# Keys and queries turned by VectorE in 32x32 blocks after a trip through DRAM, and sums of the output projection that wait for the heads

## The chip, the core and the metric

The kernel runs on one core of a Trainium2 chip. The core has five engines with a queue each, which works strictly in order: TensorE (PE; its weight loads are listed as PEld), VectorE (DVE), ScalarE (ACT), GpSimd (POOL) and SyncE (SP), which here only issues transfers. ScalarE issues transfers too, from the same queue that holds its casts. Instructions of different engines are ordered by semaphores alone. The metric is the device time of one execution in microseconds; lower is better.

## The reference

Two layers of a diffusion backbone over 256 latent tokens and 256 context tokens, 2048 channels wide, in float32. Layer 0 projects both streams by one wide matrix and runs two kinds of heads side by side: 16 attention heads of width 128 (keys and queries are normalised per head; scores of the 256 latent keys get a bias and a window mask, the 256 context keys none) and 8 groups of a state-space scan in both directions. Their gated outputs are concatenated, projected by `w_out`, gated and added to x. Layer 1 is a gated short convolution with its own two projections. Cut to what matters here:

```python
q = rms_norm(heads(cols(p, COL_Q, ...)), q_norm_g)      # 256 tokens x 16 heads x 128
k = rms_norm(heads(cols(p, COL_K, ...)), k_norm_g)      # latent, and kc from the context
s = einsum('qhd,khd->hqk', q, [k, kc]) * dh ** -0.5 + bias, masked
ya = softmax(s) @ [v, vc] * silu(gate_a)
yb = group_rmsnorm((ssd(...) + d * xs) * silu(z)) * g
x = x + gate * (concatenate([ya, yb]) @ w_out)          # then layer 1
```

## The kernel before

Every float32 product of a projection is made of three matmuls on rounded pairs: activations are split into `hH` and `hL`, weights into `wH` (a cast by ScalarE, L409) and `wL` (the rest, a subtraction by VectorE, L416). Weight tiles of 128x1024 come by SP's queue into five `raw` buffers and are split three tiles ahead (`wH0..2`, `wL0..2`). TensorE runs through the weight tiles in a fixed order: keys, values and queries of head quarter 0, then gates and the state-space columns of quarter 0, then for each quarter a = 1, 2, 3 queries, keys, gates, values and state-space columns, then `w_out` in three passes (the first over two column blocks), then layer 1.

What stands between the weight tiles is written as Python generators (`kq_gen`, `head_gen`, `make_x`, `group_gen`, `mix_gen`, `res_gen` and others). Each yields what it waits for, and a planner (`Plan`, `pump`, `force`) with its own table of costs decides after each small batch of projection matmuls whose next instructions are put into the queues. Three lists (`urgent`, `side`, `back`) are tried in this order. Where the projection itself needs something that no generator has made yet, `force` puts in the generators' instructions one after another, with no projection row between. Ten buffers `tmp` (128x512) and nine `half` (128x256) are shared under a budget: a generator begins or grows only while the budget has room.

The generators that the change and the prediction touch, with lines of the kernel before:

- `kq_gen` (L930): for each 128-token tile of keys (4) or queries (2) of a quarter, ScalarE squares the four heads (L936), VectorE and GpSimd make the inverse roots (L554, L555), VectorE scales the tile into a `tmp` (L945), and once the heads of the quarter before are done (`attn`), TensorE turns the four 128x128 squares (L202, four to a tile). ScalarE copies a key tile into `KT` (L962), VectorE scales a query tile by `gqk` into `QT` (L964). So there are 24 tiles in all.
- `head_gen` (L995): casts and low parts of the head's keys and queries (L1041 to L1045), two halves of scores, softmax, four turns for each half, their split into `PH` and `PL` (L1065, L1067), values (L1074, L1076), the product PV and the gate (L1087). The output goes to DRAM (`mixd`, L921).
- `group_gen` (L1335): for each of two halves and two heads, decay rows are loaded from DRAM (`csr`, L1356), shifted by ScalarE (L1366), subtracted by VectorE (L1370), raised by ScalarE (L1373), masked products are made (L1376 on ScalarE, L1381 and L1384 on VectorE), and TensorE multiplies them with `xtm`; sums and gates (L1396, L1398), squares (L1400). Then the group norm: L1407, a small matmul, L1418, GpSimd L1420, L1424, a matmul, L1434, and the write to `mixd`.
- `mix_gen` (L1511): a pair of 128x256 blocks is read back from `mixd` by a transfer that ScalarE issues (L1516) and split (L1521, L1522) into `mix0` to `mix31`, the activations of the output projection. Blocks 0 to 15 come from the heads, 16 to 31 from the state groups; the projection takes them in the order 0 to 11, 16 to 31, 12 to 15.
- `res_gen` (L1541): loads gate row and x for a 512-column block, gates the projection's sum and adds x. It held four `tmp` from the ninth of the sixteen steps of a pass on.

Of the kernel before, what the change touches and what calls it, by code (L numbers as in the profile page):

```python
# [37 lines left out]
class Plan:  # L38
# [32 lines left out]
    def cost(self, e, op, i, ins, outs):  # L71
        n = max(self.size(a) for a in ins + outs)
        if e == "PE":
            n, cols = self.size(outs[0]), outs[0].ap[0][1]
            if i.is_transpose:
                return n / 1.2 + 3, 190
            if ins[0].dtype == F32R:
                return 9 + 0.434 * n, 190
            return 2 * max(55, n / 1.2) * (0.27 if cols == 32 else 0.52 if cols == 64 else 1) + (80 if cols < 128 else 0), 190
        if e == "DVE":  # L80
            if op == "Memset":
                return n * 0.26 + 60, 90
            if op in ("Reciprocal", "TensorReduce"):
                return n * 1.04 + 70, 90
            if len([a for a in ins if self.size(a) >= n]) >= 2 or op == "ISA" or self.psum(ins):
                return n * 1.22 + 70, 90
            return n * 0.6 + 130, 90
        if e == "ACT":
            return n * 0.85 + 150 + (200 if len(outs) > 1 else 0), 100
        if e == "POOL":  # L90
            return (n * 186 if n < 70 else n * 2.4) + 150, 60
        return 60, 0
# [49 lines left out]
def kernel(ctx: ExitStack, tc, x, cx, ada_w, ada_b, w_in, w_out, sc_in, sc_out, rpb, small, const,  # L142
# [57 lines left out]
    def turn(o, i):  # L200
        k = i.shape[0]
        E(T.transpose(o, i, ident if k == 128 else ident[:k, :k]))  # L202


    urgent, side, back = [], [], []
    got = set()
# [720 lines left out]

    attn = [0]

    def kq_gen(key, a, ps, nt, stat, dst, banked):  # L930

        for t in range(nt):
            yield W_("ACT", ps[t])
            jk = tmp()
            for h in range(4):
                E(S.activation(jk[:, h * 128:h * 128 + 128], ps[t][:, h * 128:h * 128 + 128], AF.Square,  # L936
                               accum_out=stat[:, 4 * t + h:4 * t + h + 1]))
            give(free_t, jk)
        yield W_("DVE", stat)
        rstd(stat[:, :4 * nt], stat[:, :4 * nt], 128, EPS, 4 * nt)  # L940
        kns = {}

        def norm(t):
            kn = kns[t] = tmp()
            E(V.tensor_tensor(out=four(kn), in0=ps[t].rearrange("p (h d) -> p h d", h=4),  # L945
                              in1=stat[:, 4 * t:4 * t + 4].unsqueeze(2).to_broadcast([128, 4, 128]), op=ALU.mult))
            if banked:
                give(free_b, ps[t])

        for t in range(nt):  # L950
            yield W_("DVE", stat)
            norm(t)
        yield when(lambda: not (attn[0] < 8 * (a if key else 0)))
        for t in range(nt):
            yield W_("PE", kns[t], nb=1)
            pt = bank()
            for h in range(4):
                turn(pt[:, h * 128:(h + 1) * 128], kns[t][:, h * 128:(h + 1) * 128])
            give(free_t, kns[t])
            yield W_("ACT" if key == "K" else "DVE", pt)  # L960
            if key == "K":
                E(S.copy(dst[:, :, t * 128:(t + 1) * 128], four(pt)))  # L962
            else:
                E(V.tensor_scalar(out=dst[:, :, t * 128:(t + 1) * 128], in0=four(pt), scalar1=gqk, scalar2=None, op0=ALU.mult))  # L964
            give(free_b, pt)
        got.add((key, a))

    def v_gen(a, ps):
# [26 lines left out]
    def head_gen(a, h):  # L995
# [43 lines left out]
        yield ("grow", 2, 0)  # L1039
        yield W_("ACT", KT[:, h, :], QT[:, h, :])  # L1040
        E(S.copy(kH, KT[:, h, :]))  # L1041
        E(S.copy(qH, QT[:, h, :]))
        yield W_("DVE", kH)
        E(V.tensor_tensor(out=kL, in0=KT[:, h, :], in1=kH.bitcast(F32), op=ALU.subtract))
        E(V.tensor_tensor(out=qL, in0=QT[:, h, :], in1=qH.bitcast(F32), op=ALU.subtract))  # L1045
        yield W_("PE", kL, qL, nb=1)
        p0 = score(0)
        yield W_("DVE", p0)
# [489 lines left out]
    passed = set()  # L1538
    at = [0]

    def res_gen(k, c0, ps):  # L1541
        cols = slice(c0, c0 + 512)
        yield when(lambda: n_back[0] >= 3)
        yield W_("SP", mrow[0:1])
        g2 = []
        for t in range(2):
            yield when(lambda: at[0] >= 9 + 3 * t or k in passed)
            gb, xr = tmp(), tmp()
            E(DMA.dma_start(gb, mrow[0, cols].partition_broadcast(128)))
# [129 lines left out]
    kcol = 0  # L1679
    for ns in ((0, 512), (1024,), (1536,)):  # L1680
        pss = [banks(2) for n in ns]
        for ip in range(16):
            at[0] = ip
            if ip >= 14:
                reserve[0] = 2
            if ip == 8:
                for k, (n, ps) in enumerate(zip(ns, pss)):
                    spawn(urgent, res_gen(kcol + k, n, ps), 4)
            force(lambda: mH[2 * order[ip] + 1] is not None)
            hold[0] = len(passed) == 3 and ip >= NTAIL  # L1690
            if hold[0]:

                if ip > NTAIL:
                    continue
                force(lambda: all(mH[2 * order[q] + 1] is not None for q in range(NTAIL, 16)))
                ws = [use(q) for q in range(16 - NTAIL)]
                spawn(urgent, norm_gen(), 0, 1)
                for t in range(2):
                    for q, (H, Lo) in enumerate(ws):
                        for b in range(2):  # L1700
                            i = 2 * order[NTAIL + q] + b
                            mm_act([pss[0][t]], mH[i][:, 0, t * 128:(t + 1) * 128], mH[i][:, 1, t * 128:(t + 1) * 128],
                                   H[:, b], Lo[:, b], False, NTAIL + q == 15 and b == 1)
# [181 lines left out]
```

## Time and profile before

| | before |
|---|---|
| median of 3 runs (lowest to highest) | 1805.11 us (1805.0 to 1809.3) |
| profiled execution, its own time | 1800.62 us |
| its span | 1798.8 us |
| TensorE busy / idle in the span | 1765.1 / 33.7 us |
| VectorE, ScalarE busy | 1302.0, 796.7 us |
| turns of a `tmp` by TensorE (L202) | 324, of which 96 belong to `kq_gen` |
| granted TensorE clock | 0.999 |

The profile describes one execution, which the profiler recorded. Busy times are taken as the union of an engine's instructions; matmuls overlap each other, so that the time a matmul costs TensorE is the distance of its start from the next start, not its duration. Issues of transfers and waits in an engine's queue are not busy time. In rows by time the columns are start, time from the first start to the last end of the row, engine, line, operation, output and inputs, count, and in brackets the idle time before it with what ended it. In rows by stretch the columns are the stretch, its length, and the busy time of PE, PEld, DVE, ACT and POOL with the instruction counts, then granted clock, DMA share and GB/s.

### The profile page before, as it was taken

How to read it: one execution, taken by the hardware profiler on the slowest of the kernel's cores; microseconds unless marked ns; L12 is line 12 of the kernel's file. 1: busy time of each engine (PE TensorE's matmuls, PEld its weight loads, DVE VectorE, ACT ScalarE, POOL GpSimd, SP SyncE). 2: the span in 40 equal slices, each digit the busy share in tenths (PEclk: the TensorE clock that was granted, in tenths of full speed). 3: DMA queues.
4: the chain of work that ended last, by engine and by line, in shares of the span. 5: the costliest groups of instructions: out<-in, count | busy, mean ns of one | idle time of the engine just before them, and what ended most of it. 6: DMA issues, size and time to landing. Idle time of an engine off the chain costs nothing.

```text
span 1798.8 us, 26647 instructions
## 1 busy us (share of the span) xinstructions
PE 1765.1 (98%) x10057; PEld 1493.6 (83%) x10057; DVE 1302.0 (72%) x2121; ACT 796.7 (44%) x1410; POOL 31.1 (2%) x28
## 2 busy tenths in 40 slices
PE   6999999999999999999999999999999999999998
PEld 4677888888888879888888898888878888888887
DVE  5566777878686877685875787787657777777665
ACT  5322544436252455242454343654445444444442
POOL 0000100001000000000001000000000000000000
PEclk9999999999999999999999999999999999999999
DMA  9987654566656556655574566878857777877564
GB/s 343 343 289 256 194 168 126 156 205 196 201 171 190 156 184 200 191 157 167 171 218 119 163 190 194 233 218 286 282 182 229 242 247 226 263 224 247 188 210 153
DMA packets 249217, 376.92 MB, mean 210 GB/s; under 512 B 32656, under 2 KB 104048, under 8 KB 249088
## 3 DMA queue, kind: packets, MB, share of 16 engines
q1 hardware_dynamic: 239792, 366.64, 65.5%
q10 hardware_dynamic: 9296, 8.57, 1.4%
q8 instruction: 79, 1.29, 0.3%
q14 instruction: 50, 0.41, 0.1%
HBM read 368.70 MB, written 7.77 MB: 209 GB/s over the span
## 4 chain that ended last, share of the span: by engine, by line
PE 91%; DMA 3%; DVE 3%; issue 1%; ACT 1%; SPq 0%; POOL 0%; POOLq 0%; DVEq 0%; ACTq 0%
PE bank L198 89%; PE bank L202 3%; DMA tmp<-dram_csr 2%; DVE wL L416 1%; DMA raw<-in_ada_w 0%; DMA tmp<-dram_mixd 0%; DVE acc L803 0%; DMA tmp<-in_x 0%; DVE hL L752 0%; SPq L566 0%; DVE tmp L1381 0%; DVE tmp L1200 0%; ACT wH L409 0%; DVE half L1396 0%; DVE tmp L748 0%
## 5 line engine op out<-in xcount | busy, mean ns | idle before, releaser
L409 ACT CAST wH<-raw 128x1024 fp32r<-128x1024 f32 (+1 forms) x440 | 459.1, 1044 | 684.7 <-PE bank L198 585.5
L416 DVE TENSOR_TENSOR wL<-raw,wH 128x1024 fp32r<-128x1024 f32 (+1 forms) x440 | 531.9, 1214 | 227.0 <-ACT wH L409 224.3
L198 PE MATMUL bank<-h,wH 128*128 128x512 f32 x1024 | 358.7, 395 | 2.7 <-ACT h L1664 1.5
L198 PE MATMUL bank<-hH,wH 128*128 128x256 f32 (+1 forms) x1040 | 343.2, 330 | 0.9 <-ACT wH L409 0.9
L198 PE MATMUL bank<-hL,wH 128*128 128x256 f32 (+1 forms) x1040 | 337.2, 324 | 0.0
L198 PE MATMUL bank<-hH,wL 128*128 128x256 f32 (+1 forms) x1024 | 331.7, 324 | 1.1 <-DVE wL L416 1.1
L198 PE MATMUL bank<-h,wL 128*128 128x256 f32 x1024 | 287.2, 280 | 0.1
L198 PE MATMUL bank<-wH,hH 128*128 128x512 f32 x640 | 257.4, 403 | 4.8 <-ACT hH L746 2.6
L198 PE MATMUL bank<-wL,hH 128*128 128x512 f32 x640 | 250.1, 391 | 0.3 <-DVE wL L416 0.3
L198 PE MATMUL bank<-wH,hL 128*128 128x512 f32 x640 | 249.8, 391 | 0.1
L803 DVE SCALAR_TENSOR_TENSOR acc<-raw,csil,acc 128x512 f32<-128x512 f32 x256 | 191.8, 749 | 59.8 <-DMA raw<-in_ada_w 45.4
L198 PEld LDWEIGHTS bank<-h,wH 128*128 128x128 f32 x1024 | 192.2, 188 | 48.4 <-issue 2.6
L198 PEld LDWEIGHTS bank<-hH,wH 128*128 128x128 f32 x1040 | 197.9, 190 | 18.7 <-issue 2.0
L198 PEld LDWEIGHTS bank<-hL,wH 128*128 128x128 f32 x1040 | 198.0, 190 | 15.4
L198 PEld LDWEIGHTS bank<-hH,wL 128*128 128x128 f32 x1024 | 194.8, 190 | 17.5 <-DVE wL L416 2.1
L198 PEld LDWEIGHTS bank<-h,wL 128*128 128x128 f32 x1024 | 193.6, 189 | 0.4 <-DVE wL L416 0.4
L198 PE MATMUL bank<-wH,mix 128*128 128x512 f32 x512 | 162.8, 393 | 0.0
L198 PEld LDWEIGHTS bank<-wH,hH 128*128 128x128 f32 x640 | 120.3, 188 | 35.3 <-issue 6.6
L198 PEld LDWEIGHTS bank<-wH,hL 128*128 128x128 f32 x640 | 120.2, 188 | 25.4 <-DVE hL L752 0.6
L198 PEld LDWEIGHTS bank<-wL,hH 128*128 128x128 f32 x640 | 120.3, 188 | 24.6 <-DVE wL L416 1.1
L198 PEld LDWEIGHTS bank<-wH,mix 128*128 128x128 f32 x512 | 96.2, 188 | 20.7 <-issue 0.9
L198 PE MATMUL bank<-wL,mix 128*128 128x512 f32 x256 | 99.9, 390 | 0.0
(259 smaller groups left out, 1790.1 us busy)
## 6 DMA issues: line engine op xcount, KB each, us to landing
raw<-in_w_in SPq DMA_DIRECT2D x209, 512.0 KB
raw<-in_ada_w SPq DMA_DIRECT2D x163, 512.0 KB
raw<-in_sc_in SPq DMA_DIRECT2D x128, 512.0 KB
raw<-in_w_out SPq DMA_DIRECT2D x64, 512.0 KB
raw<-in_sc_out SPq DMA_DIRECT2D x32, 512.0 KB
tmp<-dram_csr SPq DMA_DIRECT2D x32, 256.0 KB
PT<-in_ada_w SPq DMA_DIRECT2D x14, 512.0 KB
yi<-in_ada_w SPq DMA_DIRECT2D x8, 512.0 KB
```

Source lines behind the costliest of these rows:

```text
L198: E(T.matmul(o, l, r, start=start, stop=stop, skip_group_check=True))
L202: E(T.transpose(o, i, ident if k == 128 else ident[:k, :k]))
L409: E(S.copy(H, v))
L416: E(V.tensor_tensor(out=Lo, in0=v, in1=H.bitcast(F32), op=ALU.subtract))
L803: E(V.scalar_tensor_tensor(out=acc, in0=v[:, j], scalar=csil[:, 2 * k + j:2 * k + j + 1], in1=acc, op0=ALU.mult, op1=ALU.add))
```

## The change

The tile that VectorE scales is now written with its 32-column blocks in another order (`mixed`, `plain`), goes to a DRAM buffer `kqd`, issued from ScalarE's queue (L968 of the changed kernel), and comes back two tiles at a time into one buffer `kqD` by four transfers of 32 partitions each (`fetch`, L212), also from ScalarE's queue, so that each 32x32 block lies where its turned form belongs. VectorE then turns all blocks of a tile with one instruction (`blocks`, L217) straight into `KT` or `QT`. A flag `kqbusy` lets one fetch be under way at a time. The scaling of queries by `gqk` moves into the head's cast and low part, and the tile's buffer is given back when the write is issued. The sums of the output projection (`res_gen`) are entered without a claim on buffers; they begin when all heads and groups are done and then claim four `tmp`.

```diff
+    mixed = lambda ap: ap.rearrange("p (b k i) -> p k b i", b=4, k=4)
+    plain = lambda ap: ap.rearrange("p (k b i) -> p k b i", b=4, k=4)
+    def fetch(dst, src):
+        n = src.shape[0] // 32
+        for b in range(4):
+            E(DMA2.dma_start(dst[32 * b:32 * b + 32].rearrange("p t (a x) -> p (t a) x", a=4),
+                             bass.AP(tensor=src.tensor, offset=src.offset + 128 * b, ap=[[512, 32], [32 * 512, n], [1, 128]])))
+    def blocks(o, i):
+        E(V.transpose(o.rearrange("p k (a j) -> p a k j", a=4), i.rearrange("p (a k j) -> p a k j", a=4, k=4)))
...
-            E(V.tensor_tensor(out=four(kn), in0=ps[t].rearrange("p (h d) -> p h d", h=4),
-                              in1=stat[:, 4 * t:4 * t + 4].unsqueeze(2).to_broadcast([128, 4, 128]), op=ALU.mult))
+            E(V.tensor_tensor(out=mixed(kn), in0=plain(ps[t]),
+                              in1=stat[:, 4 * t:4 * t + 4].unsqueeze(2).unsqueeze(3).to_broadcast([128, 4, 4, 32]), op=ALU.mult))
...
+            yield W_("AQ", kn)
+            E(DMA2.dma_start(src[t * 128:(t + 1) * 128], kn))
+            give(free_t, kn)
+        yield ("cap", 0, 0)
         yield when(lambda: not (attn[0] < 8 * (a if key else 0)))
-        for t in range(nt):
-            yield W_("PE", kns[t], nb=1)
-            pt = bank()
-            for h in range(4):
-                turn(pt[:, h * 128:(h + 1) * 128], kns[t][:, h * 128:(h + 1) * 128])
-            give(free_t, kns[t])
-            yield W_("ACT" if key == "K" else "DVE", pt)
-            if key == "K":
-                E(S.copy(dst[:, :, t * 128:(t + 1) * 128], four(pt)))
-            else:
-                E(V.tensor_scalar(out=dst[:, :, t * 128:(t + 1) * 128], in0=four(pt), scalar1=gqk, scalar2=None, op0=ALU.mult))
-            give(free_b, pt)
+        for t in range(0, nt, 2):
+            yield when(lambda: not kqbusy)
+            kqbusy.append(1)
+            yield W_("AQ", src[t * 128:(t + 2) * 128])
+            Dk = st([128, 2, 512], "kqD", name=f"kqD_{key}{a}{t}")
+            fetch(Dk, src[t * 128:(t + 2) * 128])
+            for k in range(2):
+                yield W_("DVE", Dk)
+                blocks(dst[:, :, (t + k) * 128:(t + k + 1) * 128], Dk[:, k])
+            kqbusy.pop()
...
-        E(S.copy(qH, QT[:, h, :]))
+        E(S.mul(qH, QT[:, h, :], gqk))
...
-        E(V.tensor_tensor(out=qL, in0=QT[:, h, :], in1=qH.bitcast(F32), op=ALU.subtract))
+        E(V.scalar_tensor_tensor(out=qL, in0=QT[:, h, :], scalar=gqk, in1=qH.bitcast(F32), op0=ALU.mult, op1=ALU.subtract))
...
+    side_left = lambda: [t for t in side if t.gen.__name__ in ("head_gen", "group_gen")]
     def res_gen(k, c0, ps):
-        yield when(lambda: n_back[0] >= 3)
+        yield when(lambda: n_back[0] >= 3 and attn[0] == 32 and not side_left())
+        yield ("grow", 4, 0)
...
-                    spawn(urgent, res_gen(kcol + k, n, ps), 4)
+                    spawn(urgent, res_gen(kcol + k, n, ps))
```

The planner's own cost of the block turn is entered as that of a reduction of the same size. Since the planner sees other instructions and other free buffers, it orders most generators' work anew from the first keys on. Three places matter below.

The first is TensorE's queue during the gates of quarter 0, where the keys of quarter 0 are turned (`const` holds the identity, `tmp` the scaled tile):

```order
 L198 MATMUL bank_124<-hL_992,wH_136 128x256
 L198 MATMUL bank_124<-hH_987,wL_139 128x256
-L202 MATMUL bank_130<-const,tmp_109 128x128 x4
-L202 MATMUL bank_129<-const,tmp_110 128x128 x4
-L202 MATMUL bank_130<-const,tmp_112 128x128 x4
 L198 MATMUL bank_123<-hH_1128,wH_137 128x256
 L198 MATMUL bank_123<-hL_1133,wH_137 128x256
```

The groups of four turns are gone and nothing stands in their place; over the whole queue 24 such rows go, and every other row is kept, many at another place.

The second is TensorE's queue at the last two state groups (6 and 7) in the first pass of the output projection. Before, the last group's products with `xtm`, its sum of squares (`half7`) and its norm (`half8`) stand apart, with rows of the projection (`mix`) between:

```order
L198 MATMUL bank7_130<-wH2_138,mix19_9248 128x512
L198 MATMUL bank4_127<-tmp5_109,xtm_147 64x128
...
L198 MATMUL bank1_124<-wH2_138,mix19_9248 128x512
...
L198 MATMUL bank0_123<-const_153,half7_121 128x1 x2
L198 MATMUL bank7_130<-wH1_137,mix21_9307 128x512
...
L198 MATMUL bank2_125<-wH2_138,mix23_9242 128x512
L198 MATMUL bank3_126<-half8_122,const_153 128x128 x2
L198 MATMUL bank7_130<-wH0_136,mix22_9239 128x512
```

In the changed kernel:

```order
L198 MATMUL bank5_128<-wH1_137,mix27_9210 128x512
L198 MATMUL bank3_126<-tmp1_105,xtm_147 64x128
...
L198 MATMUL bank7_130<-PH_1686,vH_1690 128x256
...
L198 MATMUL bank6_129<-tmp8_112,xtm_147 64x128
...
L198 MATMUL bank4_127<-tmp4_108,xtm_147 64x128
...
L198 MATMUL bank3_126<-const_153,half4_118 128x1 x2
L198 MATMUL bank7_130<-half8_122,const_153 128x128 x2
L198 MATMUL bank6_129<-tmp2_106,xtm_147 64x128
...
L198 MATMUL bank4_127<-const_153,half5_119 128x1 x2
L198 MATMUL bank3_126<-half6_120,const_153 128x128 x2
L198 MATMUL bank2_125<-wH2_138,mix28_9950 128x512
```

All four products of groups 6 and 7 (four rows each), the product PV of the last head and both norms now stand between the last row of mix27 and the first of mix28, and no row of the projection among them.

The third is ScalarE's queue ahead of mix28, the first block of group 6. Before, the read of its pair (into `tmp6`) is issued ten rows ahead of the cast; in the changed kernel it stands behind the writes of both groups:

```order
L935 DMA dram_mixd_1684<-half1_115 128x256
L935 DMA dram_mixd_1684<-half0_114 128x256
L1416 ACTIVATE half2_116<-half3_117 128x256
L935 DMA dram_mixd_1684<-half7_121 128x256
L1532 DMA tmp1_105<-dram_mixd_1684 128x2x256
L935 DMA dram_mixd_1684<-half3_117 128x256
L1532 DMA tmp5_109<-dram_mixd_1684 128x2x256
L1537 CAST mix28_9950<-tmp1_105 128x256
```

The read into `tmp1` holds group 6 alone (`half1` and `half0`), but it is issued after the write of `half7`, which is group 7's.

More of the change, by code (lines that the diff above doesn't have):

```diff
@@ L82, in cost @@
                 return n * 0.26 + 60, 90
-            if op in ("Reciprocal", "TensorReduce"):
+            if op in ("Reciprocal", "TensorReduce", "StreamTranspose"):
                 return n * 1.04 + 70, 90
@@ L928 @@
     attn = [0]
+    kqd = drt([4, 768, 512], "kqd")
+    kqbusy = []
     def kq_gen(key, a, ps, nt, stat, dst, banked):
@@ L940, in kq_gen @@
         rstd(stat[:, :4 * nt], stat[:, :4 * nt], 128, EPS, 4 * nt)
-        kns = {}
-        def norm(t):
-            kn = kns[t] = tmp()
-            E(V.tensor_tensor(out=four(kn), in0=ps[t].rearrange("p (h d) -> p h d", h=4),
-                              in1=stat[:, 4 * t:4 * t + 4].unsqueeze(2).to_broadcast([128, 4, 128]), op=ALU.mult))
+        src = kqd[a, 512 * (key == "Q"):512 * (key == "Q") + 128 * nt]
+        for t in range(nt):
+            yield W_("DVE", stat)
+            kn = tmp()
+            E(V.tensor_tensor(out=mixed(kn), in0=plain(ps[t]),
+                              in1=stat[:, 4 * t:4 * t + 4].unsqueeze(2).unsqueeze(3).to_broadcast([128, 4, 4, 32]), op=ALU.mult))
             if banked:
                 give(free_b, ps[t])
-        for t in range(nt):
-            yield W_("DVE", stat)
-            norm(t)
+            yield W_("AQ", kn)
+            E(DMA2.dma_start(src[t * 128:(t + 1) * 128], kn))
+            give(free_t, kn)
+        yield ("cap", 0, 0)
         yield when(lambda: not (attn[0] < 8 * (a if key else 0)))
-        for t in range(nt):
-            yield W_("PE", kns[t], nb=1)
-            pt = bank()
-            for h in range(4):
-                turn(pt[:, h * 128:(h + 1) * 128], kns[t][:, h * 128:(h + 1) * 128])
-            give(free_t, kns[t])
-            yield W_("ACT" if key == "K" else "DVE", pt)
-            if key == "K":
-                E(S.copy(dst[:, :, t * 128:(t + 1) * 128], four(pt)))
-            else:
-                E(V.tensor_scalar(out=dst[:, :, t * 128:(t + 1) * 128], in0=four(pt), scalar1=gqk, scalar2=None, op0=ALU.mult))
-            give(free_b, pt)
+        for t in range(0, nt, 2):
[8 more added lines that the diff above has]
+            kqbusy.pop()
         got.add((key, a))
```

## The prediction

> **What bounds the kernel now.** I read the page's busy table and its slices first, then the busy time by stretch, to see where TensorE is not working.
>
> ```profile
> span 1798.8 us, 26647 instructions
> PE 1765.1 (98%) x10057; PEld 1493.6 (83%) x10057; DVE 1302.0 (72%) x2121; ACT 796.7 (44%) x1410; POOL 31.1 (2%) x28
> PE   6999999999999999999999999999999999999998
> ...
> core 0: us, PE busy (x) PEld busy (x) DVE busy (x) ACT busy (x) POOL busy (x), PEclk, DMA share, GB/s
> 0.00:100.00 100.00, 79.09 (x575) 55.34 (x576) 57.86 (x139) 45.20 (x93) 2.91 (x10) 1.00 0.96 335
> ...
> 300.00:400.00 100.00, 100.00 (x585) 86.04 (x584) 84.30 (x148) 46.52 (x91) 2.07 (x1) 1.00 0.58 173
> ...
> 1100.00:1200.00 100.00, 99.14 (x497) 82.28 (x496) 80.78 (x166) 58.92 (x122) 0.73 (x1) 1.00 0.74 217
> ...
> 1300.00:1360.00 60.00, 56.59 (x295) 46.84 (x294) 36.61 (x57) 28.04 (x43) 1.11 (x2) 1.00 0.59 188
> ...
> 1600.00:1799.00 199.00, 193.40 (x998) 164.62 (x996) 125.98 (x160) 83.34 (x108) 0.00 (x0) 0.99 0.64 204
> ```
>
> TensorE is the bound. It is idle 21 us in the first 100, 3.4 us around 1340 and 5.6 us in the last stretch; elsewhere there is hardly a gap, at granted clock 1.00. So two things alone can move the end: TensorE work that goes away, and new holes in TensorE. Other engines' added work costs nothing unless it makes a hole. This holds as long as the order gives TensorE something to do while a head or a state group runs its long chain on VectorE and ScalarE, as between 1100 and 1200.
>
> **What is removed.** 24 groups of four turns on TensorE (16 of keys, 8 of queries), a copy by ScalarE behind each key group and a scaling by VectorE behind each query group. One group among matmuls of 256 columns, and the two followers:
>
> ```profile
> 215.20 0.29 PE L198 MATMUL bank<-hH,wL 128*128 128x256 f32 x1
> 215.32 0.60 PE L202 MATMUL bank<-const,tmp 128*128 128x128 f32 x4
> 215.68 0.36 PE L198 MATMUL bank<-hH,wH 128*128 128x256 f32 x1
> 215.88 0.28 PE L198 MATMUL bank<-hL,wH 128*128 128x256 f32 x1
> ...
> L962 ACT COPY KT<-bank x16: 585/588/599, 216.0 to 978.0; 128x512 f32<-128x512 f32 x16
> ...
> L964 DVE TENSOR_SCALAR QT<-bank,gqk x8: 742/746/752, 223.2 to 916.6; 128x512 f32<-128x512 f32 x8
> ```
>
> Starts are what counts, since ends overlap. From 215.32 to 215.68 the turns hold TensorE 0.36 us, and the next step takes 0.20 in place of 0.12, so a group costs 0.44 us, and 24 of them 10.6 us. TensorE is the bound there, so this is the gain: **-10.6 us**.
>
> **What is added, off the path.** VectorE gets 24 block transposes, which this trace does not have. The nearest rows of a 128x512 tile are 0.69 (the row at 1156.71 below) and 0.75 us (L964), so 16.6 to 18 us; 6.0 us of scaling goes away. Net some 11 us, spread over 200 to 1000, where VectorE is at most 84% busy (300 to 400): hidden by TensorE's matmuls, and 11 us if that cover were gone. The scaling that moves into a head's cast and low part makes no new instruction. ScalarE loses 16 x 0.59 = 9.4 us and issues 24 writes and 48 fetches at about 0.38 us each (L1516 below), 27 us: net +18 us on an engine 47% busy in its 100 us row. These issues wait in its queue for VectorE's product or for the write's landing, and the weight casts stand behind them. Three weight tiles, each 12 matmuls of 0.23 us or 2.8 us, are ready ahead, so a late transfer must exceed some 8 us to reach TensorE; the landings below end at 7.4. I take 0, and 7 us as the upper bound (twelve fetches at about 0.6). Of bytes, 12.6 MB more pass at a DMA share of 0.58.
>
> **What is moved.** The order is made anew by the planner, and this is where I expect the loss. In the changed order, TensorE has no projection row between the first row of the state groups' last products (tmp1) and mix28: the two groups' chains and the last head's product stand alone, and mix28 needs a read that ScalarE issues behind the write of half7, the end of the second group's chain. Before, 18 rows or more of output projection stood behind each step of the last group. VectorE's list runs in order from the first masked product of tmp1 to the scaling of half7, and cannot start early: it stands behind the softmax of head 15, which needs scores that TensorE made 24 matmuls earlier. Its prices:
>
> ```profile
> 388.38 0.64 DVE L1381 SCALAR_TENSOR_TENSOR tmp<-tmp,dtl,tmp 128x128 f32<-128x128 f32 x2 [0.78 <-ACT tmp L1376]
> 389.05 0.43 DVE L1384 TENSOR_TENSOR tmp<-tmp 128x256 f32<-128x256 f32 x1
> 396.64 1.22 DVE L416 TENSOR_TENSOR wL<-raw,wH 128x1024 fp32r<-128x1024 f32 x1
> 399.22 0.42 DVE L1396 TENSOR_TENSOR half<-bank,yi 128x256 f32<-128x256 f32 x1
> 399.67 0.42 DVE L1398 TENSOR_TENSOR half<-half,sz 128x256 f32<-128x256 f32 x1
> 414.92 0.42 DVE L1407 TENSOR_TENSOR half<-half,half 128x256 f32<-128x256 f32 x1
> 418.15 0.15 DVE L1418 TENSOR_SCALAR r<-bank 128x2 f32<-128x2 f32 x1
> 418.22 0.74 DVE L803 SCALAR_TENSOR_TENSOR acc<-raw,csil,acc 128x512 f32<-128x512 f32 x1
> 419.55 0.48 DVE L1424 TENSOR_SCALAR half<-const,r 128x128 f32<-128x128 f32 x2 [0.59 <-POOL r L1420]
> 420.94 0.87 DVE L1434 SCALAR_TENSOR_TENSOR half<-half,small,bank 128x256 f32<-128x256 f32 x2
> ...
> 438.45 0.87 DVE L1434 SCALAR_TENSOR_TENSOR half<-half,small,bank 128x256 f32<-128x256 f32 x2
> ...
> 1156.71 0.69 DVE L1067 TENSOR_TENSOR PL<-bank,PH 128x512 fp32r<-128x512 f32 x1 [0.28 <-ACT PH L1065]
> ...
> 386.96:419.95 32.99, 32.71 (x189) 26.12 (x188) 25.26 (x61) 21.38 (x72) 1.13 (x1) 1.00 0.62 170
> ```
>
> Counted in VectorE's list: 15 pairs of 128x128 x 0.64 = 9.6; 8 products x 0.43 = 3.4; 2 weight tiles x 1.22 = 2.4; 3 low parts of the head x 0.69 = 2.1; 8 of 0.42 behind the banks = 3.4; 4 more of that size = 1.7; 2 x 0.15, 2 x 0.74, 2 x 0.48 and three of the 0.87 pair's halves = 4.1. Sum **26.7 us** with no wait. But it goes to and fro with ScalarE, TensorE and the row loads: in the stretch of groups 0 and 1 (last row) VectorE was busy 25.26 of 32.99 us. At that ratio 26.7 becomes **34.9 us**. Bounds: 26.7 below; above, the 50.1 us from 388.38 to 438.45 that these two groups took from the same point to the same point. I take 34.9, since the list holds only a little beside the groups.
>
> Then the read:
>
> ```profile
> 1103.67 0.37 ACTq L1516 DMA_DIRECT2D tmp<-dram_mixd  x1
> 1106.33 0.71 ACT L1521 CAST mix<-tmp 128x256 fp32r<-128x256 f32 x2 [0.55 <-DMA tmp<-dram_mixd]
> ...
> 1209.22 0.38 ACTq L1516 DMA_DIRECT2D tmp<-dram_mixd  x1
> 1216.98 0.41 ACT L1521 CAST mix<-tmp 128x256 fp32r<-128x256 f32 x1 [4.37 <-DMA tmp<-dram_mixd]
> ```
>
> Two issues 0.8 us, landing 2.3 to 7.4 us after the issue (both times ScalarE stood waiting for it), of which I take the middle, 4.8, and a cast of 0.4: from VectorE's first row to mix28 34.9 + 0.8 + 4.8 + 0.4 = 40.9 us. TensorE's own work in it:
>
> ```profile
> 1120.34 0.66 PE L198 MATMUL bank<-tmp,xtm 128*64 128x128 f32 x8
> ...
> 1193.83 0.39 PE L198 MATMUL bank<-wL,mix 128*128 128x512 f32 x1
> 1194.06 0.62 PE L198 MATMUL bank<-wH,mix 128*128 128x512 f32 x2
> ...
> 1195.65 0.28 PE L198 MATMUL bank<-PH,vH 128*128 128x256 f32 x1
> 1197.05 0.40 PE L198 MATMUL bank<-wH,mix 128*128 128x512 f32 x1
> ```
>
> Eight turns 0.9, three matmuls 0.7, sixteen xtm products 1.3, the twelve of PV 1.4 (1195.65 to 1197.05), eight small ones 0.8: 5.1 us. The hole is **35.8 us**. What is late next is mix30: its cast stands behind that of mix14, whose read takes the buffer mix28 frees. 0.8 (two low parts) + 0.4 + 4.8 + 1.2 (three casts) = 7.2 us against 24 matmuls x 0.23 = 5.5: 1.7 us more (0 to 4.3). The restart costs something too:
>
> ```profile
> 26.34 0.74 PE L198 MATMUL bank<-wH,hH 128*128 128x512 f32 x2 [1.23 <-ACT hH L746]
> ...
> 30.00 0.49 PE L198 MATMUL bank<-wL,hH 128*128 128x512 f32 x1
> ```
>
> After the gaps of the opening, fourteen matmuls took the 3.66 us from 26.34 to 30.00, 0.26 each in place of 0.23: 0.5 us. The Trainium skill (TensorE: Matmul & The Clock Gate, The HAM clock gate) has half speed after an idle window of about 3.4 us, until a busy one has passed; by that rule the restart would be some 1.7 us, an estimate from its window, and the time 1.2 us longer. The clock granted in the opening reads 1.00, so the row does not show the halving.
>
> The second edit (the sums wait until heads and groups are done) frees four buffers early and moves eight loads of the gate and x into the hole, on SP's queue. The sums are first due when the pass ends, 96 matmuls or 22 us after mix28: hidden.
>
> **The sum.** -10.6 + 35.8 + 1.7 + 0.5 = **+27.4 us**. On the profiled execution (1800.6 us, of them 1.8 outside the span of 1798.8) it makes 1828.0; the runs' median, 1805.1, lies 4.5 higher, so the median of the changed kernel should be near **1832.5 us**.
>
> **The rivals.** (a) *The change does what it says and no hole opens*: VectorE runs far enough ahead that TensorE finds mix28 ready; 1805.1 - 10.6 = 1794.5. It decides from the point where the hole is under 10.6 us, that is, where the list's 26.7 us starts 25 us earlier against TensorE. For it: between 1100 and 1200 the same chains cost TensorE 0.9 us. Against it: those had projection rows behind them, and the scores bind the start. (b) *The two balance*: a hole of 5 to 16 us; less than the 25.1 us that 26.7 + 0.8 + 2.3 + 0.4 - 5.1 gives at the least; about 1805. (c) *The groups go at the pace of groups 0 and 1*, 50.1 us, with slow reads: 50.1 + 0.8 + 7.4 + 0.4 - 5.1 = 53.6, and 4.3 behind it; 1805.1 - 10.6 + 53.6 + 4.3 + 0.5 = 1852.9. For it: two row loads are issued late, behind SP's weight load. Against it: those 50 us held other urgent work. (d) *The fetches hold ScalarE or VectorE in order* and TensorE runs out of weight tiles while keys turn: the forecast and 7 us, 1839.5.
>
> **How the numbers follow.** Forecast 0.66, (a) 0.08, (b) 0.05, (c) 0.11, (d) 0.10. The forecast's bounds are 1819 (hole of 25.1, no second wait) and 1853. I give 1816 to 1851. A measurement here tells 0.3% (5.4 us) from nothing: faster is (a), 0.08; the same is (b), 0.05; slower is the rest, 0.87.
>
> **What would show it.** Right: TensorE idle of 30 to 40 us in one place near 1190 to 1240, released by ScalarE's cast of mix28 after the read from mixd; VectorE's busy time 8 to 14 us up; the stretches 200 to 1100 shorter by about 10 us in all, with TensorE still full. Wrong: TensorE at 99% through that place, or holes between 200 and 1000 behind the fetches, or TensorE work that did not shrink by some 10 us.

## The result, and the profile after

The changed kernel takes 1856.95 us (median of 4 runs, 1854.8 to 1859.3) against 1807.2 us (4 runs, 1805.0 to 1812.1) before: a ratio of 1.0274, 95% interval 1.0254 to 1.0294. Slower was forecast, but 1832.5 us, with a range that ended at 1851. The loss is 50 us where 27 were predicted.

The profiled execution of before (span 1798.8) lies some 7 us under its median and that of after (span 1852.7) some 2 us under, so the two profiles differ by 53.9 us where the medians differ by 49.8. The account below is that of the profiles. First the changed kernel's page: span, busy time of the engines, TensorE in 40 slices and the clock granted to it.

```profile
span 1852.7 us, 26579 instructions
PE 1774.6 (96%) x9961; PEld 1497.6 (81%) x9961; DVE 1310.3 (71%) x2137; ACT 790.3 (43%) x1394; POOL 31.7 (2%) x28
PE   6999989999999999999999999975999999999998
PEclk9999989999999999999999999986999999999999
```

TensorE has 96 matmul records fewer than before and yet is busy 9.5 us longer: it runs part of the time at a lower clock. Slices 26 and 27, counted from 0 (some 1200 to 1300 us), hold the hole; a smaller dent stands in slice 5. The next view is the busy time by stretch of the changed kernel (columns as in the prediction: length, PE, PEld, DVE, ACT, POOL, granted clock, DMA share, GB/s).

```profile
200.00:300.00 100.00, 91.78 (x528) 80.71 (x527) 67.80 (x108) 39.84 (x96) 6.36 (x2) 0.93 0.68 200
400.00:500.00 100.00, 96.84 (x548) 82.55 (x547) 68.96 (x124) 40.66 (x97) 5.19 (x3) 0.98 0.73 212
900.00:1000.00 100.00, 96.57 (x495) 79.95 (x494) 73.60 (x131) 41.15 (x113) 5.68 (x3) 0.98 0.72 212
1100.00:1200.00 100.00, 96.28 (x447) 78.72 (x447) 66.75 (x107) 39.09 (x65) 0.00 (x0) 0.98 0.72 228
1200.00:1300.00 100.00, 71.25 (x338) 57.48 (x337) 67.10 (x141) 40.76 (x83) 1.83 (x2) 0.80 0.62 181
200.00:1200.00 1000.00, 980.54 (x5537) 844.40 (x5536) 732.49 (x1228) 424.24 (x832) 25.85 (x14) 0.99 0.64 190
```

and the last of these rows for the kernel before:

```profile
200.00:1200.00 1000.00, 996.40 (x5748) 859.99 (x5747) 757.75 (x1309) 452.88 (x910) 26.34 (x15) 1.00 0.61 181
```

So there are two losses. One is the hole, where it was forecast. The other lies between 200 and 1200: TensorE is idle 19.5 us there in place of 3.6, where the prediction had it still full.

**The hole.** TensorE's timeline of the changed kernel, from the last projection rows ahead of the hole to mix28 (in brackets: idle time before the row, and what ended it):

```profile
1235.09 0.40 PE L198 MATMUL bank<-wH,mix 128*128 128x512 f32 x1
1235.42 0.43 PE L198 MATMUL bank<-tmp,xtm 128*64 128x128 f32 x2
1239.83 0.65 PE L198 MATMUL bank<-tmp,xtm 128*64 128x128 f32 x6 [3.98 <-DVE tmp L1400]
...
1252.33 0.69 PE L198 MATMUL bank<-tmp,xtm 128*64 128x128 f32 x2 [3.79 <-DVE tmp L1400]
...
1268.94 1.19 PE L198 MATMUL bank<-half,const 128*128 128x128 f32 x4 [1.44 <-DVE half L1440]
1277.31 0.80 PE L198 MATMUL bank<-wH,mix 128*128 128x512 f32 x1 [7.18 <-ACT mix L1537]
1277.91 0.63 PE L198 MATMUL bank<-wL,mix 128*128 128x512 f32 x1
...
1281.74 0.40 PE L198 MATMUL bank<-wL,mix 128*128 128x512 f32 x1
1281.98 0.62 PE L198 MATMUL bank<-wH,mix 128*128 128x512 f32 x2
```

VectorE's list, first and last row in it, and ScalarE's cast that ends the hole:

```profile
1232.62 0.61 DVE L1397 SCALAR_TENSOR_TENSOR tmp<-tmp,dtl,tmp 128x128 f32<-128x128 f32 x2
...
1270.17 0.87 DVE L1450 SCALAR_TENSOR_TENSOR half<-half,small,bank 128x256 f32<-128x256 f32 x2 [1.19 <-PE bank L198]
```

```profile
1276.86 0.71 ACT L1537 CAST mix<-tmp 128x256 fp32r<-128x256 f32 x2 [10.88 <-DMA dram_mixd<-half]
```

From 1235.42 to 1277.31 are 41.9 us. TensorE's own work in it, at the prices of the kernel before, is some 5.8 us: 32 matmuls with `xtm` at 0.66 for eight, 2.6; PV 1.4; four rows of four small ones at 0.44, 1.8. That leaves a hole of 36.1. VectorE's list, from the first of the fifteen pairs that the prediction counted, took 38.4 us (1232.62 to 1271.04), the read and the cast behind it 6.3. The eleven matmuls from 1277.31 to 1281.74 took 4.4 us in place of 2.5 at 0.23 each, at a granted clock of 0.51 in that stretch: 1.9 us for the restart.

**The stops between 200 and 1200.** The five longest, on TensorE:

```profile
245.12 0.58 PE L198 MATMUL bank<-hH,wH 128*128 128x256 f32 x1 [3.04 <-ACT wH L423]
...
257.79 1.97 PE L202 MATMUL bank<-const,tmp 128*128 128x128 f32 x8 [3.79 <-DVE gt L999]
...
480.04 0.80 PE L198 MATMUL bank<-wL,hH 128*128 128x512 f32 x1 [3.16 <-DVE wL L430]
...
959.37 0.50 PE L198 MATMUL bank<-wL,hH 128*128 128x512 f32 x1 [3.43 <-DVE wL L430]
...
1154.67 0.50 PE L198 MATMUL bank<-wL,mix 128*128 128x512 f32 x1 [2.35 <-DVE wL L430]
```

Behind each of them, at once or within 2 us, the matmuls run at about half speed for some 2 to 4 us (128x512 0.43 in place of 0.23, 128x256 0.21 in place of 0.12). Summed over those rows: 6.3 us of projection, 1.4 of turns near 258 and 1.0 of PV near 1156, 8.7 us.

Four of the five wait for the cast (`wH`) or the low part (`wL`) of a weight tile. At 245 the cast waited for a weight load that SP issued at 237.42, behind eight loads of `bias` (228.65 to 236.7). At 480, 959 and 1154 the low part stood in VectorE's queue behind a step of L817, which had waited 2.51, 3.15 and 3.12 us for another load of weights (`ada_w`). At 959:

```profile
956.64 1.54 DVE L817 SCALAR_TENSOR_TENSOR acc<-raw,csil,acc 128x512 f32<-128x512 f32 x2 [3.15 <-DMA raw<-in_ada_w]
958.10 3.49 DVE L430 TENSOR_TENSOR wL<-raw,wH 128x1024 fp32r<-128x1024 f32 x3
```

Over the whole run these waits add up to 73.1 us of VectorE, in the kernel before to 45.4. The columns of this view are the waiting instruction and what it waited for, the total in us, the number and the longest; first the changed kernel, then the one before:

```profile
DVE acc L817 <- DMA raw<-in_ada_w: 73.1, 41, 6.9
```

```profile
DVE acc L803 <- DMA raw<-in_ada_w: 45.4, 43, 3.9
```

So at these three stops the last wait is not for keys or queries. Why VectorE waits longer for `ada_w` than before, no run shows.

| term | predicted | in the profiles |
|---|---|---|
| 24 groups of turns gone | -10.6 | -10.8 (medians of a run of its own, below) |
| hole ahead of mix28 | +35.8 | +36.1 |
| second wait at mix30 | +1.7 | 0 |
| restart behind the hole | +0.5 | +1.9 |
| stops 200 to 1200, and low clock behind them | 0 (at most 7) | +15.9 and +8.7 |
| sum | +27.4 | +51.8 of 53.9 |

The term that failed is the fifth.

### The profile page after: what moved, and what is told of

The parts are those of the page before. It is cut to its first block, busy times and chain, and to the rows that moved or that the text cites. A ratio compares the mean times of both kernels' runs of the same rounds, so it can differ in the third digit from the quotient of the medians.

```text
span 1852.7 us, 26579 instructions
## 1 busy us (share of the span) xinstructions
PE 1774.6 (96%) x9961; PEld 1497.6 (81%) x9961; DVE 1310.3 (71%) x2137; ACT 790.3 (43%) x1394; POOL 31.7 (2%) x28
## 5 line engine op out<-in xcount | busy, mean ns | idle before, releaser
L817 DVE SCALAR_TENSOR_TENSOR acc<-raw,csil,acc 128x512 f32<-128x512 f32 x256 | 191.7, 749 | 87.2 <-DMA raw<-in_ada_w 73.1
L198 PEld LDWEIGHTS bank<-hH,wL 128*128 128x128 f32 x1024 | 196.0, 191 | 19.5 <-DVE wL L430 3.8
```

The lines of the kernel that those rows point to most:

```text
L198: E(T.matmul(o, l, r, start=start, stop=stop, skip_group_check=True))
L817: E(V.scalar_tensor_tensor(out=acc, in0=v[:, j], scalar=csil[:, 2 * k + j:2 * k + j + 1], in1=acc, op0=ALU.mult, op1=ALU.add))
```

## The experiments

### What the turns are worth

The kernel before, its turns of keys and queries left out, all rows else in the same order:

```diff
-                turn(pt[:, h * 128:(h + 1) * 128], kns[t][:, h * 128:(h + 1) * 128])
+                plan.turned(...)        # booked as before, not issued
-                E(S.copy(dst[:, :, t * 128:(t + 1) * 128], four(pt)))
+                E(S.copy(dst[:, :, t * 128:(t + 1) * 128], four(kns[t])))
```

> The kernel before, without the 24 groups of turns of the keys and queries on TensorE; ScalarE's copies and VectorE's scalings read the normalised tiles where they read the turned ones, and all else stands in the same order. The heads' results are not the reference's. It measures the prediction's first term, -10.6 us (24 x 0.44). Theory: TensorE is the bound, and all of it is gained: 1795 to 1798 us where the kernel before takes 1807. Rival: part of it goes into waits that the turns had covered (VectorE and ScalarE come no sooner), -3 to -7 us; that would explain why the run with 18 tiles through DRAM was no faster than the kernel before.

Measured 1797.4 us against 1808.2 on the same chip, ratio 0.9943 (0.9922 to 0.9963): -10.8 us, by the interval 6.7 to 14.1 less, so the theory. The prediction's first term is right, and 1797 us is the least that the change could have reached if it made no new hole.

### The second edit alone

```diff
-        yield when(lambda: n_back[0] >= 3)
+        yield when(lambda: n_back[0] >= 3 and attn[0] == 32 and not side_left())
+        yield ("grow", 4, 0)
```

> The kernel before, with the second edit alone (the sums wait for heads and groups, and claim their buffers late). TensorE's rows stand in the same order as before. Theory: nothing, 0 +- 3 us against the kernel before. Rival: the loads of gate and x that now come late cost at the end of the first pass, 3 to 8 us slower.

Measured 1807.3 us, ratio 0.999 (0.9976 to 1.0004): nothing. Alone the second edit costs nothing; whether it costs something beside the first is tried further down.

### Keeping TensorE busy in the hole

```diff
             py = bank()
+            warm(py, s, 16)     # 16 turns of the identity, last quarter only; 16 and 10 at the two later steps
```

> The changed kernel, with turns of the identity (16, 16 or 10 of them, of 0.11 us each) on TensorE ahead of each step of the last quarter's two groups, into banks that the step then overwrites; they compute nothing that is used, and the order of all else is the same. Theory C: behind a stop of some 3 us TensorE runs at half speed for a while, so that in the hole before mix28 its own work took 13 us in place of 5, and the first matmuls behind it 0.42 us in place of 0.23. Kept busy, the clock between 1200 and 1300 rises from 0.80 to over 0.9, mix28 to mix30 start at full speed (2.1 us saved), and the time is 2 to 8 us under the changed kernel's. Rival: the clock is not what costs there, the groups' chain on VectorE and ScalarE is, and the 116 turns (13 us) stand in the way of TensorE's steps: no difference, or up to 4 us more.

Measured 1859.2 us, ratio 1.0285 (1.0265 to 1.0304), which overlaps the changed kernel's interval: no difference, the rival. The busy view of the hole, of the changed kernel and then of this one, in which it lies some 5 us later:

```profile
1236.00:1277.30 41.30, 12.72 (x58) 9.37 (x58) 24.71 (x66) 15.40 (x43) 1.83 (x2) 0.56 0.51 142
```

```profile
1241.00:1282.50 41.50, 24.58 (x178) 21.01 (x176) 24.98 (x66) 16.24 (x46) 1.83 (x2) 0.85 0.49 149
...
1282.51 0.80 PE L198 MATMUL bank<-wH,mix 128*128 128x512 f32 x1 [8.31 <-ACT mix L1545]
```

The clock is up from 0.56 to 0.85, and the hole is nearly as long: from the start of the last projection row to mix28 it is 41.5 us (1240.98 to 1282.51), in the changed kernel 42.2 (1235.09 to 1277.31). TensorE's slow work in the hole costs next to nothing, since the groups' chain on VectorE and ScalarE sets its length. The restart is not saved either: the last wait, 8.3 us, comes after the last step that could be filled.

### Other rows into the hole

```diff
-    order = list(range(0, 6)) + list(range(8, 16)) + [6, 7]
+    order = list(range(0, 6)) + list(range(8, 14)) + [6, 7, 14, 15]
```

> The changed kernel, with the pairs of the output projection in another order: the pairs of the last quarter's heads (6 and 7) ahead of those of its groups (14 and 15). The same is computed. Theory A: the hole before mix28 is as long as the two groups' chain on VectorE and ScalarE, and the rows of pairs 6 and 7, 48 matmuls of 0.23 us or 11 us, can now run in it: the hole falls by 8 to 11 us, 1846 to 1850 us. Rival B: the heads' products stand in the same late list as the groups', so pairs 6 and 7 come no sooner, or the groups move back by what is put ahead of them: 1853 to 1861 us.

Measured 1854.8 us, ratio 1.0251 (1.023 to 1.0273), 2 us under the changed kernel, whose interval it overlaps: the rival. TensorE now stops twice ahead of rows of the projection, at 1260 and at 1290:

```profile
1260.42 0.79 PE L198 MATMUL bank<-wH,mix 128*128 128x512 f32 x1 [2.97 <-ACT mix L1537]
...
1290.36 0.80 PE L198 MATMUL bank<-wH,mix 128*128 128x512 f32 x1 [12.33 <-ACT mix L1537]
```

The last heads are as late as the last groups. So the question is not what stands in the hole, but why heads and groups had moved back against the projection.

### Why they are late: how the planner books a fetch

The planner keeps times by a tile's name and a piece of its columns; partitions aren't in the key:

```
            return [(n, u) for u in range(lo // 128, hi // 128 + 1)]
...
        for k in ko:
            s = max(s, 0.0 if e == "PE" else self.w[k] + 60, self.r[k] + 60)
```

The four fetches of a pair write the same columns of four groups of 32 partitions. For the planner each overwrites the one before and has to wait for its landing, so that a pair is given four landings in a row, and ScalarE's queue with it. In the trace they run side by side. One pair of the changed kernel, its issues on ScalarE's queue, and VectorE's turns of it:

```profile
465.34 2.06 ACTq L212 DMA_DIRECT2D kqD_K<-dram_kqd  x4
```

```profile
482.17 1.30 DVE L217 STREAM_TRANSPOSE KT<-kqD_K 128x512 f32<-128x512 f32 x2
```

The DMA records of the trace have the last packet of this pair at 472.7 us, and VectorE's list comes to the tile 9.5 us later. Over the twelve pairs it took 3.3 to 12.6 us from the first issue to the last packet, 7.3 in the mean. Booked as running together:

```diff
+            if b:
+                plan.par = {dst.tensor.name}
...
-            s = max(s, 0.0 if e == "PE" else self.w[k] + 60, self.r[k] + 60)
+            s = max(s, 0.0 if e == "PE" or k[0] in self.par else self.w[k] + 60, self.r[k] + 60)
```

> The changed kernel, with one rule of the planner other: the four fetches of a pair of tiles, which write four different groups of 32 partitions, are booked as running together, where the changed kernel books each behind the landing of the one before (in its order a pair is given about four times the time of one fetch; in its trace the packets of a pair have all landed 3.3 to 12.6 us after the first issue). Nothing that is computed differs. Theory A: the hole before mix28 is made by the order, since keys are booked far later than they come; heads and groups then stand late against the projection. A expects rows of output projection again behind the last groups' steps, no hole of more than 5 us near 1200 to 1280, and about 39 us less than the changed kernel: 1815 to 1825 us, with the short stops between 200 and 1200 still there (16 us of idle time and what the lower clock costs behind them). Rival B: the trip through DRAM itself is that long, and an order that asks for the keys earlier only moves the wait ahead of the heads' scores: TensorE idle in new places at the scores, 1845 to 1860 us.

Measured 1836.1 us, ratio 1.0157 (1.0136 to 1.0178), 21 us under the changed kernel. This lies between the two ranges and in neither. Heads and groups come earlier, as A has it (the last group's product with `xtm` at 1242 us, in the changed kernel at 1264, before the change at 1202), but a stop of 12.7 us is left at the end of the list, where A allowed none over 5, and some of what rival B said is seen too (4.4 us at the scores of the second quarter, 473 us). Between 200 and 1200 TensorE is idle as long as in the changed kernel, 19.6 us in place of 19.5, at other places; so the booking has to do with the hole and not with the sum of those stops. TensorE, and ScalarE's queue ahead of it:

```profile
1264.37 0.80 PE L199 MATMUL bank<-wH,mix 128*128 128x512 f32 x1 [12.68 <-ACT mix L1541]
```

```profile
1252.29 0.81 ACTq L939 DMA_DIRECT2D dram_mixd<-half  x2
1259.13 0.41 ACTq L1536 DMA_DIRECT2D tmp<-dram_mixd  x1
1263.91 0.71 ACT L1541 CAST mix<-tmp 128x256 fp32r<-128x256 f32 x2 [11.59 <-DMA tmp<-in_x]
```

The last pair goes through DRAM: 6.8 us from its write to the issue of the read, 4.8 to the cast.

The same with the sums of before:

> As the run before, and the sums of the output projection as in the kernel before the change (they claim four buffers when they are spawned and don't wait for heads and groups). Theory A: the second edit is worth nothing once the heads are in time: within 3 us of the run before. Rival: the four buffers that the sums hold early are missing to the last heads and groups, 5 to 15 us slower than the run before.

Measured 1833.3 us, ratio 1.0145 (1.013 to 1.016): the intervals of the two overlap, and no effect of the second edit shows here either. The loss belongs to the first edit.

With the last heads' pairs ahead of the last groups' on top (the edit of `order` above):

> The fetches of a pair booked together as in the run that did this alone (1836.1 us, with a stop of 12.7 us ahead of mix30, whose read waits for the landing of its write), and the pairs of the last heads ahead of those of the last groups. Theory A: the 11 us of rows cover that stop: 1823 to 1828 us. Rival: the write and the read of the last pair come later by as much: 1833 to 1838 us.

Measured 1822.8 us, ratio 1.0082 (1.0061 to 1.0103): theory A. The stop of 12.7 us is 0.6. The order that gave 2 us while the heads were late gives 13 once they are early.

The control, that order in the kernel before:

> The kernel before, with the pairs of the last heads ahead of those of the last groups, as a control for the runs that have this order. There TensorE has rows left behind the last groups' steps in either order. Theory: no difference, 1807 +- 3 us. Rival: the other order alone gains or loses 5 us or more, and what the runs with it gained isn't from the fetches.

Measured 1808.6 us, ratio 1.0008 (0.9995 to 1.0021): no difference, so the 13 us are not from the order alone.

### What makes the stops between 200 and 1200

First, fetches with packets of 4 KB in place of 512 B:

```diff
-                             bass.AP(tensor=src.tensor, offset=src.offset + 128 * b, ap=[[512, 32], [32 * 512, n], [1, 128]])))
+                             bass.AP(tensor=src.tensor, offset=src.offset + 32768 * b, ap=[[1024, 32], [1, 1024]])))
```

> The changed kernel, with each fetch reading 32 pieces of 4 KB in a row in place of 256 pieces of 512 B: as many bytes, as many issues, the same waits and the same order on all engines; the keys and queries that arrive are in wrong places, so the heads' results are not the reference's. Theory D: the stops between 200 and 1200 us (16 us, and the lower clock behind them) come from the fetches' 12,288 packets of 512 B on the 16 engines that also carry the weights: the fetches then land in half the time, the stops near 245, 480 and 959 us shrink, 1843 to 1850 us. Rival: they come from the order in which ScalarE, VectorE and the weight queue stand behind each other: within 3 us of the changed kernel's 1857.

Measured 1856.3 us, ratio 1.026 (1.0241 to 1.0279): the rival. The fetches didn't land in half the time as the theory had it; from first to last packet a pair took 4.8 us in the mean in place of 5.4, with an eighth of the packets. So the number of packets is not what holds them, and the stops at 245, 258, 481 and 964 us are still there.

Then the booking, 4.5 us longer than in the run of 1822.8 us:

```diff
-                done = free = max(self.dma, s + 1000) + n / self.RATE + 1500
+                done = free = max(self.dma, s + 1000) + n / self.RATE + 1500 + (4500 if ko[0][0].startswith('kqD') else 0)
```

> As the run before, with the landing of a fetch booked 4.5 us later (a pair then has about 9 us from the first issue; in the trace of the changed kernel the twelve pairs took 3.3 to 12.6 us, 7.3 in the mean). Theory A: with the keys booked too early, TensorE's list has the scores ahead of their data (a stop of 4.4 us near 473 us, others of 1 to 3 us); booked as they land, these stops go: 1815 to 1822 us. Rival: the stops are not from the booking but from late weights and row loads, and they stay: within 4 us of the run before.

Measured 1813.7 us, ratio 1.0034 (1.0021 to 1.0048): 9 us less, beyond what A expected. But the stop that A named is not gone:

```profile
478.38 0.80 PE L199 MATMUL bank<-kH,qH 128*128 128x512 f32 x1 [2.09 <-ACT qH L1062]
```

(4.4 us, then 2.8, then 2.1 in the profiles of the three runs; the profiled execution of the last took 1819.8 us, 6 over its median.) Here too one number in the planner moves many rows; that the 9 us come from the scores is not shown.

Last, the first quarter. In the changed kernel its four tiles of keys go through DRAM in two pairs, one behind the other. VectorE's turns of them, and what TensorE waited for at 257.79:

```profile
236.72 1.30 DVE L217 STREAM_TRANSPOSE KT<-kqD_K 128x512 f32<-128x512 f32 x2
...
250.66 1.29 DVE L217 STREAM_TRANSPOSE KT<-kqD_K 128x512 f32<-128x512 f32 x2
...
257.06 0.67 DVE L999 SCALAR_TENSOR_TENSOR gt<-tmp,bank 128x512 f32<-128x512 f32 x1
```

The gate's step (L999) may only start once the first keys are there (`a or ("K", 0) in got`), and holds a bank that the turn at 257.79 needs. The writes left at 215 us; the keys are there 37 us later. Turned by TensorE as before in the first quarter alone, the other 18 tiles through DRAM:

```diff
+        if (key, a) in {("K", 0), ("Q", 0)}:
+            ...        # the turns and copies of the kernel before
+            return
         src = kqd[a, 512 * (key == "Q"):512 * (key == "Q") + 128 * nt]
```

> As the run that booked fetches 9 us long (1813.7 us), with the first quarter's six tiles of keys and queries turned by TensorE as before the change and the other 18 through DRAM and VectorE. Theory A: the stops of 3.1 and 1.3 us near 238 and 244 us, where B's turns and their sources wait while the first keys and queries are on their way, go, with some 1.5 us of low clock behind them; the six groups of turns cost 6 x 0.44 = 2.6 us: 3 us less, 1808 to 1812 us. Rival: the stops there are not from the first keys but from the gate's and B's chains on VectorE, and stay: 1814 to 1818 us.

> As the run beside it, with fetches booked 2 us longer still (about 11 us a pair). Theory A: scores that meet their keys late (a stop of 2.1 us near 478 us) go: 1805 to 1810 us. Rival: a longer booking than the landings makes the heads later than need be and a stop ahead of the last mixes returns: 1812 to 1825 us.

Measured 1806.0 us, ratio 0.9988 (0.9976 to 1.0000), and with the longer booking 1806.5 us, ratio 0.9993 (0.9982 to 1.0004). The first is 8 us under the run without it, more than A's 3; the second adds nothing. Its stretches:

```profile
200.00:300.00 100.00, 99.50 (x625) 88.75 (x624) 76.68 (x137) 52.28 (x122) 5.45 (x2) 1.00 0.59 177
...
200.00:1200.00 1000.00, 992.05 (x5686) 852.33 (x5685) 774.94 (x1333) 447.62 (x891) 27.56 (x15) 1.00 0.65 196
1200.00:1300.00 100.00, 99.59 (x467) 81.81 (x466) 71.72 (x94) 46.66 (x66) 0.70 (x1) 1.00 0.82 278
```

Hole and first stops are gone, the clock is at 1.00, and the 50 us are given back. TensorE's idle time between 200 and 1200, 18.2 to 19.6 us in the four runs with the booking changed and all quarters through DRAM, falls to 8.0; the stops at 238 and 244 were 4.4 of these 10 us, and the rest went with rows that moved, so what of it is the keys' trip alone is not shown. It is level with the kernel before and not faster: 18 of 24 groups of turns should bring 8.1 us by the first experiment, 4.4 go into idle time that is left between 200 and 1200 (8.0 us against 3.6), and the other 3 are not located.

## Why the prediction was right or wrong

- *TensorE is the bound, so only its own work and new holes count*: right, as far as the account above goes (51.8 of 53.9 us).
- *-10.6 us for the turns*: right, -10.8 alone.
- *The hole of 35.8 us between the last mix27 row and mix28*: right in its place in the queue and in mechanism. The size, 36.1, is right partly by luck. VectorE's list took 38.4 us in place of 34.9, and the issues, read and cast 6.3 in place of 6.0, 3.8 more. TensorE's own work beside it was 8.6 us in place of 5.1: the products with `xtm` are 32 matmuls in the trace where 16 were priced, the small ones 16 where 8 were, and 2.8 us of rows ran at the start of the list where 1.6 were counted. The two errors cancel. Part of the longer list is what rival (c) named: ScalarE waited 2.6 and 1.8 us for decay rows (`csr`) at 1249 and 1256. Of the reason for the hole the prediction knew only the order as it stood. That much of it came from a wrong booking, as the run at 1836 us shows, it didn't ask.
- *1.7 us at mix30*: wrong, no wait there.
- *0.5 us for the restart*: wrong, 1.9, and some 1 to 3 behind each earlier stop. The row of the opening that the estimate came from runs at granted clock 1.00 and was the wrong row. The Trainium skill (TensorE: Matmul & The Clock Gate, The HAM clock gate) has half speed until a busy window of about 3.4 us has passed; the 1.7 us worked out from it is an estimate, and the trace is close to it with 1.9.
- *The fetches: "I take 0, and 7 us as the upper bound"*: this is the step that failed. TensorE, forecast still full between 200 and 1200 us, has 15.9 us more idle time there and 8.7 us of low clock behind the stops. The term had four faults. The landing was taken from reads of 2.3 to 7.4 us, while pairs of fetches took up to 12.6 and went one pair after another, so that the first keys came 37 us after their writes. The cover was counted for weight casts behind ScalarE's issues alone (8 us); at 258 us it was a bank that was missing, held by a step that waits for the keys. That VectorE's low parts stand in order behind other loads was left out: at 480, 959 and 1154 us the three tiles of cover were used up while VectorE waited for `ada_w`. And a stop was priced at its idle time, without the matmuls behind it. Rival (d) had the kind of stop, weight tiles that are not ready, with the same 7 us; that the fetches are what holds them is not shown, and at 1154 us no fetch had been issued for 130 us. Rival (c)'s 1852.9 is near the result, but its cause, groups at 50 us, didn't occur.
- *The second edit costs nothing*: right.
- *The range*: its upper end stood on one hole; nothing in it allowed for several short stops.

What stays open: why VectorE waits longer for `ada_w` than before the change (the fetches' packet size doesn't do it), how far the time moves with any small change of a booking (4.5 us more on the booked landing of each fetch moved it by 9), and where 3 of the 8 us go that the last version should have gained.

## What to carry to other kernels

Where an order is written by a planner, an edit's first cost is what the planner believes of the new instructions: four DMAs that write different partitions of one tile ran side by side here, and were four in a row to this planner. Booking them together gave back 21 of the 50 us, and 34 together with another place for the last pairs. When a change sends data that many steps wait for through DRAM, count what those steps hold (banks, buffers) until it is back, and price each stop of the bound engine with the slow restart behind it. Ask too what stands in order behind the loads that come later: here a step that only adds up waited for its load and held the weights of the engine that sets the time. A hole that is as long as another engine's chain isn't shortened by work for the idle engine.

## What the runs showed of the hardware

A stop of 1.75 us can already cost the clock. In the kernel before without its turns:

```profile
414.70 0.61 PE L215 MATMUL bank<-const,half 128*128 128x1 f32 x4 [1.75 <-DVE half L1426]
...
415.49 0.37 PE L215 MATMUL bank<-hH,wL 128*128 128x256 f32 x1
415.66 0.42 PE L215 MATMUL bank<-hH,wH 128*128 128x256 f32 x1
415.88 0.42 PE L215 MATMUL bank<-hL,wH 128*128 128x256 f32 x1
...
419.06 0.28 PE L215 MATMUL bank<-hL,wH 128*128 128x256 f32 x1
```

After 1.75 us of idle time the next few matmuls still follow each other at 0.12 to 0.17 us, and from 415.66 to 418.8 at 0.21, half speed. The Trainium skill (TensorE: Matmul & The Clock Gate, The HAM clock gate) has half speed after at least one idle window of about 3.4 us; here a stop of half that length was enough (the same after 1.75 us at 387 us in the run of 1836 us). Not every such stop does it: in the run of 1806.0 us stops of 1.88 and 2.00 us (410.55, 1150.44) are followed by 0.23 for a 128x512 matmul, one of 1.34 us (745.51) by 0.43 from 747.6 on. What decides between them is not shown. And twelve pairs of fetches landed in nearly the same time with 4 KB packets as with 512 B ones (4.8 against 5.4 us from first to last packet): an eighth of the packets bought little, and what sets the time was not tried.
